# Durations that a hand-written planner uses for matmuls, ScalarE squares and GpSimd operations, and a scratch tile taken out of its ordering

## Chip, core and metric

The kernel runs on one NeuronCore of a Trainium2 chip. The metric is device time in microseconds (us) of that core, from the launch to the end of the program. The profile's own span, from the first to the last instruction of the program, is a little shorter.

## The reference, cut to what matters

Two layers work on a sequence of 256 tokens of width 1024, all in float32. Each layer has three parts, and each part normalises its input, normalises its result and adds it to the residual x:

```
for l in range(2):
    h = rms_norm(x, ln_mix_pre[l]); z = h @ w_in[l]             # 1024 x 7436
    branches = nsa(z), retention(z), rwkv7(z), short_conv(z)    # four token mixers
    merged = sum over m of sigmoid(z_gate[m]) * (branches[m] @ w_branch[l, m])
    x = x + rms_norm(merged @ w_mix_out[l], ln_mix_post[l])
    x = x + rms_norm(cross_attention(rms_norm(x, ...), rms_norm(mem, ...)), ln_xa_post[l])
    h = rms_norm(x, ln_mlp_pre[l])
    x = x + rms_norm(square(relu(h @ mlp_w1[l])) @ mlp_w2[l], ln_mlp_post[l])
```

`rms_norm` needs the mean square of each row, then its power of -1/2. These few numbers stand between the last matmul of one part and the first matmul of the next.

## The kernel before, in words

**Tiling.** Tokens are two tiles of 128 (t = 0 and 1). Weights stream in as units of 128 x 1024 numbers. Each is split by ScalarE (`hi`, rounded to float32r) and VectorE (`lo`, the rest), and each product is three float32r matmuls (`mm3`: hi hi, hi lo, lo hi), of 256 or 512 columns. The second matmul of the MLP uses a seven-product scheme in place of eight; its weights need sums too, one of them made by a DMA that adds (`accumulate`, line 738, issued from GpSimd's queue). The small matmuls of the mixers stay in plain float32, many of them on 64-row tiles, issued in groups (`together`, line 700).

**The planner.** The kernel's program is not issued in the order in which it is written. Each operation is recorded by `Sched.add` with an engine, a duration in us, and dependencies with latencies (`LAT`, `OWN`). `Sched.run` then plays a list schedule: at each step it takes the operation that can start first, by its own clock for PE, ACT, DVE, POOL and DMA; of those that start together, the one of lowest rank. Rank 9 is the stream of large matmuls, rank 0 the chain between two parts, ranks 1 to 5 the mixers and the preparation of memory, "split" a rank that depends on how many units are split ahead of use. The order in which it takes them is the order of the instructions on each engine and on each DMA queue. On the chip every engine works its list in that order and waits at its head. The planned durations are used for nothing else: they leave no trace in the program but the order.

**Durations.** They stand in the helpers: `act` (line 628), `ts` (line 649; on GpSimd where `pool=True`), `rpow` (line 672, a power on GpSimd), `mm` (line 679) and `together`, which adds up its members. In the profile all squares, copies and splits of ScalarE carry line 631, VectorE's tensor_tensor line 642, its scalar_tensor_tensor line 648, tensor_scalar of either engine line 654, GpSimd's power line 676, matmuls line 685 and transposes line 690.

**Scratch tiles.** Tiles of a tag share a number of buffers (`NB`). `Sched.fits` lets an operation start a tile only if all tiles of that tag that stand earlier in the program can still be placed. The tag `junk` has one buffer. It takes the squares themselves, which nobody reads: the sum of squares leaves through the accumulator of the same instruction. With one buffer the rule makes the squares run in the order of the program text, one after another with 0.1 us between them. The squares are in `sumsq` (line 920), `pre_first` and `post_bank` (line 1005).

**A boundary between two parts.** `wide` (the end of a mixer or of cross-attention) and the end of `mlp` finish token tile 0, then token tile 1. For each, `post_bank` squares the result's two banks of 512 columns and multiplies by the gain; `post` forms the power of -1/2 on GpSimd (two operations) and updates x on VectorE (two operations); `pre` multiplies x by the next gain, squares x, and transposes on PE for the next part. In program order tile 0's whole `boundary` stands ahead of tile 1's `post_bank`. While a boundary runs, PE has other matmuls in hand where there are any: in layer 0 the keys of the memory for both layers (`kpairs`; `ftile_whole` in plain float32 at the end of layer 0).

## Time and profile before

| what | value |
|---|---|
| median of 3 runs | 1088.1 us (1085.91 to 1088.32) |
| the profiled execution's own time | 1090.18 us |
| its span, first to last instruction | 1088.1 us |
| PE busy | 98% of the span |
| VectorE, ScalarE, GpSimd busy | 79%, 60%, 9% |
| mean granted TensorE clock | 0.998 |

PE's busy time is made of records that overlap: a matmul's record lasts longer than the distance to the next one's start. So work on PE is read below from starts, and idle PE time in a row is shorter than the stall by what the last record overhangs. Rows of the other engines say when a result was there; a number in square brackets in a row is the idle time of that engine just before it, with what ended it.

### The profile page before, as it was taken

The page shows a single profiled execution, that of the slowest core. Times are in us where ns is not written, and L with a number is a line of the kernel's source. Part 1 is how long each engine was busy: PE and PEld are TensorE (multiplying, and loading weights), DVE is VectorE, ACT ScalarE, POOL GpSimd, SP SyncE. Part 2 cuts the span into 40 slices and gives each one's busy share as a digit, 9 for nine tenths or more (in the row PEclk, how much of TensorE's full clock was granted, in tenths as well). Part 3 has the DMA queues.
Part 4 walks back from the last instruction along what each step waited for, and adds up shares of the span by engine and source line. Part 5 has one row for each costly group of instructions (what it writes and reads, how often), then busy time and mean ns, then how long its engine had stood idle before and what let it go on. Part 6 is the DMA issues. An engine that isn't in the chain of part 4 may idle for free.

```text
span 1088.1 us, 20208 instructions
## 1 busy us (share of the span) xinstructions
PE 1069.9 (98%) x7848; PEld 936.1 (86%) x7848; DVE 856.8 (79%) x1347; ACT 657.5 (60%) x1069; POOL 96.1 (9%) x154
## 2 busy tenths in 40 slices
PE   8999999999999999999999999999999999999997
PEld 7989877888998899999889998778888987999996
DVE  6867887866767689888796767977867667999997
ACT  7574655645555667776665664644546455776673
POOL 2000011001100110000020000100002002000000
PEclk9999999999999999999999999999999999999999
DMA  8546555755546699998945257356645467889981
GB/s 328 164 128 183 210 174 165 266 186 169 170 157 218 212 273 288 267 279 254 298 165 172 79 160 254 126 174 201 237 164 173 149 224 210 255 267 293 270 265 51
DMA packets 75970, 225.18 MB, mean 207 GB/s; under 512 B 12223, under 2 KB 14015, under 8 KB 75748
## 3 DMA queue, kind: packets, MB, share of 16 engines
q1 hardware_dynamic: 71268, 207.65, 55.7%
q0 software_dynamic: 4320, 15.73, 8.8%
q8 instruction: 61, 1.00, 0.4%
q10 hardware_dynamic: 288, 0.52, 0.2%
q14 instruction: 33, 0.27, 0.1%
HBM read 221.77 MB, written 3.15 MB: 207 GB/s over the span
## 4 chain that ended last, share of the span: by engine, by line
PE 88%; DMA 3%; DVE 3%; issue 2%; ACT 2%; POOL 2%; SPq 0%; POOLq 0%; DVEq 0%; ACTq 0%
PE A L685 47%; PE C L685 18%; PE S L685 12%; PE B L685 8%; DMA g<-wts 2%; PE C L690 2%; DVE g L642 1%; POOL s L654 1%; DMA raw<-wts 1%; ACT junk L631 1%; DVE lo L642 1%; DVE x L648 1%; ACT g L631 1%; PE B L690 0%; POOL s L676 0%
## 5 line engine op out<-in xcount | busy, mean ns | idle before, releaser
L642 DVE TENSOR_TENSOR lo<-raw,hi 128x1024 fp32r<-128x1024 f32 (+1 forms) x308 | 368.4, 1213 | 70.2 <-ACT hi L631 41.8
L631 ACT ACTIVATE hi<-raw 128x1024 fp32r<-128x1024 f32 (+1 forms) x308 | 316.2, 1049 | 136.7 <-PE A L685 67.1
L685 PE MATMUL A<-hi,g 128*128 128x512 f32 (+2 forms) x1152 | 370.3, 389 | 0.9 <-ACT g L631 0.5
L685 PEld LDWEIGHTS A<-hi,g 128*128 128x128 f32 x1152 | 214.5, 188 | 48.1 <-issue 4.3
L685 PE MATMUL A<-lo,g 128*128 128x512 f32 (+2 forms) x576 | 220.2, 382 | 0.0
L642 DVE TENSOR_TENSOR g<-g,g 128x512 f32<-128x512 f32 (+3 forms) x218 | 187.9, 886 | 9.8 <-ACT g L631 8.5
L631 ACT ACTIVATE g<-g 128x512 fp32r<-128x512 f32 (+7 forms) x228 | 149.0, 693 | 43.3 <-DVE g L642 19.6
L685 PE MATMUL A<-g,hi 128*128 128x256 f32 x928 | 169.2, 285 | 0.0
L685 PE MATMUL C<-g,hi 128*128 128x256 f32 x960 | 167.7, 278 | 1.1 <-ACT g L631 1.1
L685 PEld LDWEIGHTS C<-g,hi 128*128 128x128 f32 x960 | 147.4, 188 | 3.7 <-ACT g L631 1.5
L685 PEld LDWEIGHTS A<-g,hi 128*128 128x128 f32 x928 | 141.2, 188 | 5.2 <-issue 3.4
L685 PE MATMUL C<-g,lo 128*128 128x256 f32 x480 | 133.5, 278 | 0.0
L685 PE MATMUL A<-g,lo 128*128 128x256 f32 x464 | 129.1, 278 | 0.0
L631 ACT ACTIVATE g<-C 128x512 fp32r<-128x512 f32 (+5 forms) x119 | 59.4, 513 | 110.8 <-PE C L685 84.6
L685 PEld LDWEIGHTS A<-lo,g 128*128 128x128 f32 x576 | 108.4, 188 | 17.5
L685 PE MATMUL S<-g,g 128*128 128x512 f32 x450 | 108.3, 391 | 0.3 <-DVE g L642 0.3
L685 PEld LDWEIGHTS S<-g,g 128*128 128x128 f32 x450 | 84.3, 188 | 19.0 <-DVE g L642 0.8
L685 PEld LDWEIGHTS C<-g,lo 128*128 128x128 f32 x480 | 91.0, 190 | 0.0
L685 PEld LDWEIGHTS A<-g,lo 128*128 128x128 f32 x464 | 87.3, 188 | 0.2 <-DVE lo L642 0.2
L631 ACT ACTIVATE g<-A 128x512 f32<-128x512 f32 (+3 forms) x70 | 39.5, 567 | 54.4 <-PE A L685 42.3
L654 POOL TENSOR_SCALAR s<-s 128x1 f32<-128x1 f32 (+1 forms) x38 | 27.3, 719 | 349.8 <-ACT junk L631 297.1
L642 DVE TENSOR_TENSOR g<-C,g 128x512 fp32r<-128x512 f32 (+3 forms) x66 | 37.0, 587 | 23.7 <-ACT g L631 17.3
(144 smaller groups left out, 1079.0 us busy)
## 6 DMA issues: line engine op xcount, KB each, us to landing
raw<-wts SPq DMA_DIRECT2D x300, 512.0 KB, 4.7
g<-wts SPq DMA_DIRECT2D x90, 256.0 KB, 5.3
g<-wts POOLq DMA_DIRECT2D x30, 512.0 KB, 5.7
g<-rows SPq DMA_DIRECT2D x11, 512.0 KB, 4.7
g<-memT SPq DMA_DIRECT2D x12, 256.0 KB, 6.9
g<-cmpw SPq DMA_DIRECT2D x4, 512.0 KB, 4.5
raw<-wts SPq DMA_DIRECT2D x4, 498.0 KB, 6.2
raw<-wts SPq DMA_DIRECT2D x4, 480.0 KB, 6.2
```

What stands on the lines that cost most here:

```text
L631: e = lambda: self.nc.scalar.activation(real(out), real(in_), func, bias=real(bias), scale=real(scale), accum_out=real(accum))
L642: f = lambda: e.tensor_tensor(real(out), real(a), real(b), op)
L648: f = lambda: self.nc.vector.scalar_tensor_tensor(real(out), real(a), real(s), real(b), op0=op0, op1=op1)
L654: f = lambda: e.tensor_scalar(real(out), real(a), real(s1), real(s2), op0=op0, **kw)
L685: e = lambda: self.nc.tensor.matmul(real(out), real(lhsT), real(rhs), start=start, stop=stop, skip_group_check=True)
L690: self.pe(0.109, out, [in_, self.ident], lambda: self.nc.tensor.transpose(real(out), real(in_), real(self.ident)), 128)
```

## The change

Four kinds of edits. (1) The planned durations: a float32r matmul takes n/2240 in place of n/2400 + 0.002 us; a group with 64-row operands takes 0.25 us more; a tensor_scalar on GpSimd 0.7 in place of 0.15; a power on GpSimd 0.1 more. (2) An ACT operation takes 0.01 more, 0.19 more where it accumulates (0.064 before), and nothing more for a scale or bias from a tile (0.064 and 0.096 before, and 0.042 more when the input is in SBUF). (3) The scratch tile of the squares becomes one fixed tile with its own place. (4) Writes into it make no dependency (`sink`). No operation is added or removed, and none works on other data.

```diff
-NB = {..., "g1": 5, "junk": 1, "s": 14, "x8": 6,
+NB = {..., "g1": 5, "s": 14, "x8": 6,
@@ class VT
+        self.sink = False
@@ Sched.add
         for v in op.outs:
             t = v.t
+            if t.sink:
+                continue
@@ act
-        cost = 0.08 + self.free(out) / 1200 + 0.064 * n + (0.042 if n and not in_.t.psum else 0.0)
+        cost = 0.09 + self.free(out) / 1200 + 0.19 * (accum is not None)
@@ ts, on GpSimd
-            return self.s.add("POOL", 0.15 + self.free(out) / 800, [out], [a, s1, s2], f)
+            return self.s.add("POOL", 0.7 + self.free(out) / 800, [out], [a, s1, s2], f)
@@ rpow
-        return self.s.add("POOL", 0.25 + 0.2 * n, [out], [a], f)
+        return self.s.add("POOL", 0.35 + 0.2 * n, [out], [a], f)
@@ mm
-            c = max(n, 252) / 2400 + 0.002
+            c = max(n, 252) / 2240
-            c = max(n, 128) * 4 / 2400 + 0.003
+            c = max(n, 128) * 4 / 2400 + 0.004
@@ together
-            cost = i = 0
+            cost, i = 0.25 * (g[0][1].shape[0] == 64 or g[0][2][0].shape[0] == 64), 0
@@ setup
+        self.junk = self.keep([128, 512], "junk", BF16)
+        self.junk.t.sink = True
@@ sumsq, pre_first, post_bank
-            j = self.tile([128, 512], "junk", BF16)
+            j = self.junk
```

## Rows read from the trace of the kernel before

**Rows 1.** The page: busy time, share of the span and instructions of each engine.
```profile
PE 1069.9 (98%) x7848; PEld 936.1 (86%) x7848; DVE 856.8 (79%) x1347; ACT 657.5 (60%) x1069; POOL 96.1 (9%) x154
```

**Rows 2.** Busy time of each engine by stage. Columns: the stretch, its length, PE, PEld, DVE, ACT and POOL busy with their instructions, granted clock, DMA share, GB/s. In order: the mixers of layer 0; its gated sums; the end of layer 0's MLP into layer 1; the mixers of layer 1; the MLP of layer 1; the end.
```profile
9.00:180.00 171.00, 171.00 (x1727) 146.61 (x1727) 136.05 (x275) 105.89 (x204) 13.92 (x29) 1.00 0.57 190
180.00:262.00 82.00, 82.00 (x372) 67.35 (x371) 57.65 (x71) 41.53 (x57) 2.67 (x5) 1.00 0.62 212
...
540.00:580.00 40.00, 38.17 (x221) 33.35 (x220) 35.05 (x45) 26.58 (x47) 8.08 (x9) 1.00 0.62 214
580.00:740.00 160.00, 159.26 (x1628) 135.73 (x1629) 121.45 (x255) 90.62 (x176) 10.80 (x19) 1.00 0.48 154
...
922.00:1078.00 156.00, 156.00 (x1019) 142.25 (x1018) 142.90 (x198) 109.86 (x151) 11.21 (x13) 1.00 0.82 242
1078.00:1089.00 11.00, 2.05 (x15) 1.76 (x13) 6.08 (x11) 2.47 (x8) 2.71 (x5) 0.71 0.25 95
```

**Rows 3.** The chain that ended last, in the MLP of layer 0. Columns: start, length, engine, tile and line, number of pieces.
```profile
417.41 5.45 PE C L685 x48
422.87 4.78 PE S L685 x21
...
438.13 5.45 PE C L685 x48
```

**Rows 4.** Timeline of PE where the MLP of layer 0 ends and layer 1 begins. Columns: start, length, engine, line, operation, out<-in, form, count, idle time before and who ended it. B<-g,raw are the keys of layer 1 in plain float32; C<-g,g are the transposes of token tile 0, then of tile 1.
```profile
552.44 5.34 PE L685 MATMUL B<-g,raw 128*128 128x256 f32 x24
557.62 2.03 PE L685 MATMUL C<-g,g 128*128 128x128 f32 x16
559.48 5.34 PE L685 MATMUL B<-g,raw 128*128 128x256 f32 x24
566.17 2.05 PE L685 MATMUL C<-g,g 128*128 128x128 f32 x16 [1.34 <-DVE g L654]
568.06 3.62 PE L685 MATMUL B<-g,raw 128*128 128x256 f32 x16
```

**Rows 5.** Timeline of POOL in the same stretch, token tile 1.
```profile
558.02 1.42 POOL L654 TENSOR_SCALAR s<-s,s 128x1 f32<-128x1 f32 x1 [0.80 <-ACT junk L631]
559.52 0.56 POOL L676 TENSOR_TENSOR s<-s,mhalf 128x1 f32<-128x1 f32 x1
563.34 1.81 POOL L654 TENSOR_SCALAR s<-s 128x1 f32<-128x1 f32 x1 [3.26 <-ACT junk L631]
565.23 0.56 POOL L676 TENSOR_TENSOR s<-s,mhalf 128x1 f32<-128x1 f32 x1
```

**Rows 6.** Timeline of DVE in the same stretch: the two operations beside GpSimd's first and fourth row of the group above, and what PE waited for.
```profile
558.06 1.22 DVE L642 TENSOR_TENSOR lo<-raw,hi 128x1024 fp32r<-128x1024 f32 x1
...
563.85 1.22 DVE L642 TENSOR_TENSOR lo<-raw,hi 128x1024 fp32r<-128x1024 f32 x1
565.83 0.29 DVE L654 TENSOR_SCALAR g<-ident,s 128x128 f32<-128x128 f32 x1 [0.77 <-POOL s L676]
```

**Rows 7.** All tensor_scalar operations of POOL on one small tile (line 654): shortest, median and longest in ns, first and last start, forms.
```profile
L654 POOL TENSOR_SCALAR s<-s x38: 196/440/1807, 7.0 to 918.5; 128x1 f32<-128x1 f32 x34, 128x8 f32<-128x8 f32 x4
```

**Rows 8.** Timeline of PE at the transposes of token tile 1, from the mixer of layer 0 into its cross-attention, and from that into its MLP. B<-g,hi are keys of the memory.
```profile
274.88 0.28 PE L685 MATMUL B<-g,lo 128*128 128x256 f32 x1
275.38 0.66 PE L690 MATMUL C<-ident,g 128*128 128x128 f32 x4 [0.22 <-DVE g L642]
...
379.40 0.66 PE L690 MATMUL C<-ident,g 128*128 128x128 f32 x4 [0.21 <-DVE g L642]
```

**Rows 9.** Timeline of PE from the cross-attention of layer 1 into its MLP, where no keys are left.
```profile
907.37 1.26 PE L690 MATMUL C<-ident,g 128*128 128x128 f32 x8 [0.47 <-DVE g L642]
...
909.78 0.51 PE L685 MATMUL A<-hi,g 128*128 128x512 f32 x1 [0.47 <-ACT g L631]
...
910.91 0.74 PE L685 MATMUL A<-hi,g 128*128 128x512 f32 x2 [0.40 <-DVE g L642]
...
917.24 1.60 PE L690 MATMUL C<-ident,g 128*128 128x128 f32 x12 [1.01 <-DVE g L642]
```

**Rows 10.** Timeline of ACT in the same stretch. junk<-x squares token tile 0's x, junk<-A the two banks of token tile 1.
```profile
906.02 0.63 ACT L631 ACTIVATE junk<-x 128x512 bf16<-128x512 f32 x1 [3.10 <-DVE x L648]
...
909.16 1.06 ACT L631 ACTIVATE g<-C 128x512 fp32r<-128x512 f32 x2
910.11 0.59 ACT L631 ACTIVATE junk<-A 128x512 bf16<-128x512 f32 x1
...
911.63 0.59 ACT L631 ACTIVATE junk<-A 128x512 bf16<-128x512 f32 x1
```

**Rows 11.** Timeline of PE at the end of the rwkv mixer of layer 1, and at the first products of the MLP of layer 0.
```profile
676.38 0.63 PE L690 MATMUL B<-ident,g 128*128 128x128 f32 x4 [0.60 <-DVE g L642]
...
406.84 0.50 PE L685 MATMUL C<-g,hi 128*128 128x256 f32 x2 [1.11 <-ACT g L631]
```

**Rows 12.** Groups of ACT by form: two of 128 x 256 with the scale from a tile, and without. Columns: busy us, mean ns of one, idle time before.
```profile
L631 ACT ACTIVATE g<-g 128x256 f32<-128x256 f32 x62 | 23.1, 408 | 0.6
...
L631 ACT ACTIVATE g<-g,pct 128x256 f32<-128x256 f32 x12 | 5.5, 499 | 0.9 <-DVE g L648 0.8
```

**Rows 13.** The chain that ended last, in its last 6 us.
```profile
1081.84 1.04 POOL s L654
```

More of the change, by code (lines that the diff above doesn't have):

```diff
@@ L225, in body @@
         Prog(nc, tc, sb, ps, dr, wts, x, mem, memT, pc, rows, r256, cmpw, cmpe, relb, lora, cst, out, dbg).run()
-NB = {"raw": 5, "hi": 8, "lo": 8, "g8": 7, "g4": 12, "g2": 13, "g1": 5, "junk": 1, "s": 14, "x8": 6,
+NB = {"raw": 5, "hi": 8, "lo": 8, "g8": 7, "g4": 12, "g2": 13, "g1": 5, "s": 14, "x8": 6,
       "p1": 1, "tok1": 1, "tok2": 1, "lk": 1, "ng": 1}
@@ L991, in pre_first @@
                 self.red(acc[:, 0:1], sq, OP.add)
-                j = self.tile([128, 512], "junk", BF16)
+                j = self.junk
                 self.act(j, x[:, 512:], AF.Square, scale=D ** -0.5, accum=acc[:, 1:2])
@@ L1010, in post_bank @@
         cs = cs or slice(512 * i, 512 * i + 512)
-        j = self.tile([128, 512], "junk", BF16)[:, :cs.stop - cs.start]
+        j = self.junk[:, :cs.stop - cs.start]
         self.act(j, bank, AF.Square, accum=acc[:, i:i + 1])
```

## The prediction

> **What bounds the kernel now.** I read the page's busy times first: PE 98%, the next engine 79% [rows 1]. A busy PE is not proof of a full one, so I then read the stages [rows 2]: through the mixers of layer 0 (171 us) and the gated sums (82 us) PE has no idle time at all, in the mixers of layer 1 0.74 of 160 us, in the second MLP none of 156 us. Third, the chain of waits in the MLP, to see the pace of that full PE [rows 3]: from 417.41 to 438.13 are two rounds of 48 matmuls of 256 columns and 21 of 512, so 10.36 us a round. The reader is to see two things there. PE's work is fixed, and the order cannot shorten it. And the planner's old prices, 256/2400 + 0.002 = 0.1087 us and 512/2400 + 0.002 = 0.2153 us, make 48 x 0.1087 + 21 x 0.2153 = 9.74 us of that round, 6% too little; the new ones, 0.1143 and 0.2286, make 10.29 us. The price is now right to 1%.
>
> So what the change can win is idle PE: 1088.1 - 1069.9 = 18.2 us [rows 1], of which 8.1 are the tail (10.1 from 1078 us to the end of the span, less 2.05 of work [rows 2]) and 5.8 the nine waits in [rows 4, 8, 9, 11]. Fourth, therefore, the timelines around these stalls. A stall is read from start to start: a record of 256 columns overhangs the next start by 0.17 us (0.28 long, next start 0.11 later), so a stall is its idle time plus about 0.17.
>
> **The change part by part.** No instruction is added or taken away, no DMA either; everything acts through order. Each term is a stall that the order makes.
>
> *GpSimd prices.* The mean power chain at a boundary is a tensor_scalar and a power. The planner gave 0.15 and 0.45 us; it now gives 0.70 and 0.55. Into layer 1 PE ran 24 records of keys, tile 0's transposes, 24 more keys, stood for 1.34 us (stall 1.51), ran tile 1's transposes, and only then the last 16 records of keys, 3.62 us [rows 4]. The filler was there, but queued behind the transposes, because the planner thought that tile 1's x would be ready sooner. Its two GpSimd pairs took 1.42 + 0.56 and 1.81 + 0.56 us [rows 5], 4.35 in all, against 1.20 planned: 3.15 short. The new prices plan 2.50 and are 1.85 short. The plan's chain grows by 1.30, and by 0.09 for each of two squares, and a group of keys is 4 records, 0.9 us of the 3.62; so one or two groups move ahead of the transposes. I take 1.3 us of the 1.51; bounds 0 and 1.5.
>
> The same at the transposes of tile 1 into the first cross-attention and the first MLP: idle 0.22 and 0.21 us, stalls 0.39 each with the overhang, and keys follow at both [rows 8]. One GpSimd pair stands in each chain, so the plan grows by 0.65, more than the stall. I take both, 0.8 us; bounds 0 and 0.8. At the end of layer 1's rwkv mixer a pair stands in the chain too, PE waits 0.60 idle [rows 11], and the gated sums' matmuls are there as filler: 0.5 us; bounds 0 and 0.8.
>
> Here row and rule differ about the price itself. The tensor_scalar took 196 to 1807 ns, median 440 [rows 7], and the long ones end just behind a VectorE subtraction of 1.22 us: the 1.42 us one at 559.44, the `lo` beside it at 559.28; the 1.81 us one at 565.15, its `lo` at 565.07 [rows 5, 6]. No single number fits that; at a boundary 1.4 to 1.8 is near, off it 0.2 to 0.4.
> The Trainium skill (SBUF — State Buffer, Who interferes with whom) says that a VectorE instruction with two inputs in SBUF keeps out a GpSimd instruction that reads SBUF, and that whichever is issued first keeps the port to its end. The trace agrees that GpSimd waits the subtraction out, though its row starts 0.04 us ahead of it at 558.02; by that rule the price would hang on the neighbour, one group of keys (0.9 us) would move in place of 1.3 us, and the sum below would be 3.4.
>
> *The squares set free.* Into the last MLP there are no keys left, and PE waits four times: 0.47, 0.47, 0.40 and 1.01 us idle [rows 9]. The last is tile 1's transposes. Tile 1's first bank was squared at 910.11 and its second at 911.63, though ACT had stood idle 3.10 us until 906.02, when the squares of tile 0's x could begin [rows 10]. The order of the text put those ahead. Set free, the first bank's square goes into that idle time, and 0.59 us leave ACT's queue ahead of the second; the chain of tile 1 (two GpSimd operations, two on VectorE, the gain) starts that much earlier. I take 0.6 us of a stall of 1.18; bounds 0 and 1.2. The first three waits are tile 0's chain, which no square precedes that could move: nothing. Next late there is that chain. At the other boundaries the same gain is covered by the keys, and counts within the terms above.
>
> *Matmul prices.* With matmuls 5 to 6% dearer the plan hides DMA, splits and chains behind fewer of them; loads and splits keep their pace, which follows units used. Where PE waits for the MLP's first factors, 1.11 us idle [rows 11], the plan sees PE later by 6% and may take the splits in a better order, or not: bounds 0 and 1.3, half of it, 0.6 us. In the mixers it costs a reserve: until now PE in truth came 5% later to each small group than planned, so the group's inputs were nearly always there; now it comes as planned. The 0.25 us for 64-row groups acts in the same way. I cost this at nothing, since the planner's latency of 0.2 us between engines is still in every step; its bounds come under the rivals.
>
> *ACT prices.* A plain operation of 128 x 256 took 408 ns and one with its scale from a tile 499 [rows 12]; the old price had 0.106 for that difference of 0.09, the new one nothing. The new square is 0.09 dearer. The 12 in that group are spread over mixers where PE never waits: nothing, with bounds of -0.5 and +1 us (12 x 0.09).
>
> *The end.* The last GpSimd sum takes 1.04 us [rows 13] where 0.2 to 0.4 is the lower half of [rows 7]; what VectorE runs beside it depends on the order of tile 0's updates. Nothing, bounds -0.7 and +0.7.
>
> **Sum.** 1.3 + 0.8 + 0.5 + 0.6 + 0.6 = 3.8 us less. The profiled execution took 1090.18 us, with a span of 1088.1; it gives 1086.4. It lies 2.1 above the median of the runs, 1088.1, and taken from that the forecast is **1084.3 us**, 0.35% less. A measurement of this kernel can tell some 0.3%, 3.3 us, from no change.
>
> **The rivals.**
>
> *The stalls move and don't go* (within 3.3 us). Filler put ahead of one stall is missing behind it, where ACT still has to split the transposed x; and where GpSimd's operation is held up by VectorE, 0.70 is still short by 0.7 to 1.1 us each. For it: the stall into layer 1 is one of two chains whose plan stays 1.85 us short. Against it: 3.62 us of keys were left there. With half of the terms, 1.9 us, it gives 1086.2; nothing at all gives 1088.1. The variant that the change does not do what it says, since the order comes out nearly the same, ends here too: most of the time is MLP and gated sums with no idle PE [rows 2].
>
> *PE arrives too early in the mixers* (slower). The place is the rwkv chains between 20 and 135 us and between 580 and 690 us, some 225 us in the mixer stages of [rows 2], in which small groups alternate with large matmuls on PE. The price: the planner used to fill a chain's waiting time with 5.2% more matmul time than it knew (0.1143 against 0.1087). If chains run longer on the chip than planned, PE now stands at their groups: at most 5.2% of 225 = 11.7 us, half of it, 5.8, where every other step is late. It decides once a chain step is planned shorter than it runs: GpSimd beside VectorE is (up to 1.8 for 0.70), ACT with a scale is by 0.09 [rows 5, 12]. Against it: PE has no idle time there now, with a reserve of which only half is given up. It gives 1088.1 + 5.8 = 1093.9 us.
>
> **How the numbers follow.** Forecast, faster by more than 3.3 us: 0.43, since four of its five terms are stalls with filler in hand or a named delay, but it clears the bound by 0.5 us only. Moved stalls: 0.35. Early PE: 0.22. The lower end takes all named stalls, 1.5 + 0.8 + 0.8 + 1.2 + 1.3 = 5.6, the end's 0.7, ACT's 0.5 and the three waits of tile 0 with two more of their size elsewhere, 3.8: 1088.1 - 10.6 = 1077.5. The upper end is the slower rival's 1093.9, of whose case the worse half stays out. The likeliest case alone runs from 1077.5 to 1084.8.
>
> **What would show it.** After the change: 1 or 2 more groups of B<-g,raw ahead of tile 1's transposes into layer 1, and less than 0.4 us idle before them in place of 1.34; the square of tile 1's first bank ahead of the squares of tile 0's x, ACT idle under 2.5 us there in place of 3.10, and 0.4 us idle before the last transposes in place of 1.01; the MLP's round unchanged at 10.36 us; PE busy in the mixers without idle time. The forecast is wrong if PE's idle time ahead of the tail stays near 10.1 us (18.2 less 8.1), or if the mixers or their matmuls' starts spread by more than 3 us: then the planner's old error was a reserve. It is wrong in its reason if the time falls but PE idles as before and the end is shorter.

## The result, and the profile after

| | before | after |
|---|---|---|
| median of the runs shown beside each other | 1088.21 us (1085.91 to 1089.23, 4 runs) | 1101.42 us (1096.89 to 1104.61, 4 runs) |
| profiled execution, its span | 1090.18, 1088.1 us | 1102.74, 1100.9 us |

The ratio is 1.0118 with a 95% interval of 1.0096 to 1.014: the change makes the kernel 13 us slower, where 4 us less were forecast and 1093.9 us was the upper end. The runs also spread wider, over 7.7 us.

Busy time by stage of the changed kernel, with the columns of [rows 2], in four of its stretches, the last one longer: the mixers of layer 0; the end of layer 0's MLP into layer 1; the MLP of layer 1; the end.

```profile
9.00:180.00 171.00, 169.31 (x1717) 145.30 (x1718) 138.86 (x281) 105.44 (x204) 14.24 (x28) 1.00 0.54 185
...
540.00:580.00 40.00, 37.59 (x192) 32.91 (x191) 29.50 (x39) 21.88 (x38) 7.55 (x8) 0.96 0.57 196
...
922.00:1078.00 156.00, 151.73 (x992) 137.65 (x991) 140.86 (x195) 108.75 (x153) 15.49 (x16) 0.99 0.87 248
1078.00:1101.00 23.00, 14.90 (x71) 12.27 (x70) 14.63 (x23) 6.16 (x16) 2.71 (x5) 0.88 0.12 46
```

The reader is to see the third row. The last MLP had no idle PE before, 156.00 of 156.00; now 4.3 us of it are idle, and in two stretches (540 to 580, 922 to 1078) the mean granted clock is under 1. To place the loss, I compare the start of the n-th matmul record in both traces; each has 7848. Behind record 120 the changed kernel is late by 1.8 us, behind 1950 (layer 0's mixers done) by 3.5, at 3000 by 2.8, at 3750 (layer 0's MLP near its end) by 5.3, at 4200 (layer 1 begun) by 7.4, at 6900 (last MLP begun) by 7.0, at 7800 by 12.8. So the start costs 1.8 us, layer 0's mixers 1.7, the rounds of the first MLP 2.4, its end with the boundary 2.1, **the last MLP 5.8**, and the rest gives back 1.1.

That last figure is the kernel before's own execution: the profiled one lies 2.1 us above the median of its runs. In experiment 12 below PE, ScalarE, VectorE and GpSimd work in the same order as in the kernel before everywhere outside the two MLPs, and its trace is 0.2 us ahead of the kernel before's at record 1950 and 3.9 us at 6900. Against it the changed kernel gives nothing back: the start costs 2.0 us, layer 0's mixers 1.7, its sums and cross-attention 0.3, its MLP 1.9, the boundary 3.3, layer 1's mixers 1.7, the last MLP 5.3 (16.2 in all, as that execution is a short one of 1086.48 us).

What happens in an MLP round shows in three timelines of the changed kernel: ScalarE, then PE, then the DMA issues of POOL and SP. Columns: start, length, engine, line, operation, tiles, form, count, idle time before and who ended it. `g<-g` of 128x1024 are the splits of U and W (U is what the accumulating DMA writes, W is summed from it by VectorE), `g<-C` is the relu that empties the bank for the next `up`.

```profile
991.32 1.06 ACT L634 ACTIVATE g<-g 128x1024 fp32r<-128x1024 f32 x1 [3.17 <-DMA g<-wts]
993.72 1.06 ACT L634 ACTIVATE g<-g 128x1024 fp32r<-128x1024 f32 x1 [1.34 <-DVE g L645]
994.68 1.04 ACT L634 ACTIVATE hi<-raw 128x1024 fp32r<-128x1024 f32 x1
995.63 0.58 ACT L634 ACTIVATE g<-C 128x512 f32<-128x512 f32 x1
```

```profile
992.68 1.10 PE L688 MATMUL S<-g,g 128*128 128x512 f32 x4
996.26 0.50 PE L688 MATMUL C<-g,hi 128*128 128x256 f32 x2 [2.49 <-ACT g L634]
```

```profile
982.63 0.85 POOL L741 DMA_DIRECT2D g<-wts  x1 [9.54 <-DMA g<-wts]
```

```profile
982.85 0.33 SPq L731 DMA_DIRECT2D raw<-wts  x1
983.23 1.72 SPq L731 DMA_DIRECT2D g<-wts  x3
```

PE's last matmul into C started at 988.65, so the relu could have run at about 989. It stood fourth in ScalarE's queue: behind U's split, which stood 3.17 us at the head for the accumulating DMA (issued at 982.63), behind W's, which waited 1.34 us for VectorE, and behind a `hi`. PE ran out of other products and stood for 2.49 us. In the kernel before the relu of the same round comes first, as soon as PE has finished, and the splits of U (982.77) and W (984.03) follow, before PE needs the bank at 986.88:

```profile
982.28 0.60 ACT L631 ACTIVATE g<-C 128x512 f32<-128x512 f32 x1 [2.69 <-PE C L685]
982.77 2.31 ACT L631 ACTIVATE g<-g 128x1024 fp32r<-128x1024 f32 x3
```

The accumulating DMA is also later than before: in the last MLP the median from issue to landing is 7.8 us where it was 5.5 (rows of the DMA issues of 925 to 1085 us, the kernel before first, then the changed one):

```profile
g<-wts POOLq DMA_DIRECT2D x13, 512.0 KB, 5.5
...
g<-wts POOLq DMA_DIRECT2D x14, 512.0 KB, 7.8
```

The long stall has a tail. Three windows of the changed kernel, before, in and behind a stretch of half clock:

```profile
990.00:996.50 6.50, 4.01 (x19) 2.98 (x18) 5.12 (x6) 3.84 (x5) 0.86 (x1) 1.00 0.84 260
996.68:1000.09 3.41, 3.41 (x18) 3.41 (x17) 3.39 (x7) 2.55 (x5) 0.00 (x0) 0.50 1.00 262
1000.20:1003.60 3.40, 3.40 (x31) 3.40 (x31) 3.40 (x6) 2.30 (x3) 0.00 (x0) 1.00 0.94 331
```

PE was idle for 2.49 of the 6.5 us ahead; then the granted clock was 0.50 (1.2 GHz) for 3.41 us, with 18 matmuls, nearly all of them of 256 columns as in the next stretch, which has 31. So 13 of 31 are missing, some 1.4 us of work. The second such stretch lies behind the other long stall, at the boundary into layer 1 (566.60 to 570.01 us).

There PE, answering to [rows 4], and POOL, answering to [rows 5]:

```profile
557.04 7.07 PE L688 MATMUL B<-g,raw 128*128 128x256 f32 x32
566.51 3.68 PE L688 MATMUL C<-g,g 128*128 128x128 f32 x16 [2.41 <-DVE g L657]
```

```profile
561.65 1.69 POOL L657 TENSOR_SCALAR s<-s,s 128x1 f32<-128x1 f32 x1 [1.97 <-ACT junk L634]
563.42 0.85 POOL L679 TENSOR_TENSOR s<-s,mhalf 128x1 f32<-128x1 f32 x1
564.37 0.85 POOL L657 TENSOR_SCALAR s<-s 128x1 f32<-128x1 f32 x1
565.30 0.84 POOL L679 TENSOR_TENSOR s<-s,mhalf 128x1 f32<-128x1 f32 x1
```

It is now tile 0's transposes that wait, behind 32 records of keys, 2.41 us idle where tile 1's waited 1.34 us. POOL takes tile 1's first pair (561.65) ahead of tile 0's second (564.37). And the whole chain began late, in the same way as in the MLP: the first operation of the end, the copy `g<-S`, is behind two `hi` splits that waited 3.76 us for their DMAs (before, it ran at 544.01). How much of the 2.41 us is this and how much the order on POOL, no run separates.

```profile
547.94 1.06 ACT L634 ACTIVATE hi<-raw 128x1024 fp32r<-128x1024 f32 x1 [3.55 <-DMA raw<-wts]
549.22 1.06 ACT L634 ACTIVATE hi<-raw 128x1024 fp32r<-128x1024 f32 x1 [0.21 <-DMA raw<-wts]
550.18 0.58 ACT L634 ACTIVATE g<-S 128x512 f32<-128x512 f32 x1
```

**Why the plan does this.** The code's own prices say it. Per MLP round the plan charges the DMAs 3 x 1.54 us for units, 0.77 for half a unit, 2 x 0.77 for the halves of U and 3.08 for the accumulating one: 10.02 us. The round's matmuls were 9.74 us at the old price and are 10.29 at the new. So the plan's round was bound by its DMAs and is now bound by PE. While DMAs bound it, a split was planned for when its data came, and the relu was ready by then. With PE the bound, the planned DMAs run ahead, and so do the planned splits, by 4 us and more ahead of the relu. On the chip they do not run ahead: U's split above waited 3.17 us for its data. The plan also gives out the buffers, by the time at which it has one free, so a moved price moves tiles to other buffers as well as other places in the queues (the planned durations do not act through the order alone); no run separates the two. The account so far, a relu held in ScalarE's queue, is theory 1; theory 2 is the recorded rival (PE too early in the mixers); theory 3 puts the loss at the boundary, on the squares or the POOL prices.

### The profile page after: what moved, and what is told of

It reads as the page before. It is cut to its first block, busy times and chain, and to the rows that moved or that the text cites. A ratio compares the mean times of both kernels' runs of the same rounds, so it can differ in the third digit from the quotient of the medians.

```text
span 1100.9 us, 20238 instructions
## 1 busy us (share of the span) xinstructions
PE 1077.6 (98%) x7848; PEld 942.1 (86%) x7848; DVE 859.3 (78%) x1347; ACT 656.9 (60%) x1069; POOL 94.5 (9%) x154
## 4 chain that ended last, share of the span: by engine, by line
PE 77%; DVE 9%; DMA 6%; issue 4%; ACT 2%; POOL 1%; SPq 0%; DVEq 0%; POOLq 0%; ACTq 0%
PE A L688 46%; PE C L688 13%; PE B L688 9%; PE S L688 7%; DVE g L645 6%; DMA g<-wts 4%; DVE lo L645 2%; PE C L693 2%; ACT g L634 2%; DVE g L651 1%; DMA raw<-wts 1%; DMA g<-cmpw 1%; ACT hi L634 1%; PE B L693 0%; DMA x<-x 0%
## 5 line engine op out<-in xcount | busy, mean ns | idle before, releaser
L634 ACT ACTIVATE g<-g 128x1024 fp32r<-128x1024 f32 (+7 forms) x228 | 152.2, 694 | 103.1 <-DVE g L645 59.5
L688 PE MATMUL A<-g,hi 128*128 128x256 f32 x928 | 171.5, 286 | 0.6 <-DVE g L651 0.5
L688 PEld LDWEIGHTS C<-g,hi 128*128 128x128 f32 x960 | 148.3, 190 | 10.1 <-ACT g L634 8.3
L741 POOL DMA_DIRECT2D g<-wts x30 | 26.4, 879 | 319.7 <-DMA g<-wts 147.1
```

What stands on the lines that cost most here:

```text
L634: e = lambda: self.nc.scalar.activation(real(out), real(in_), func, bias=real(bias), scale=real(scale), accum_out=real(accum))
L688: e = lambda: self.nc.tensor.matmul(real(out), real(lhsT), real(rhs), start=start, stop=stop, skip_group_check=True)
L741: f = lambda: self.nc.gpsimd.dma_start(real(out), in_, accum_op=OP.add)
```

## The experiments

"Round" counts MLP rounds from 0. A stall of PE "by starts" is its idle time plus the 0.16 to 0.17 us that the last record overhangs; where a text says idle, it is the idle time alone. Stalls come from one profiled execution each. Stalls "ahead of C" are those of the kind above, released by ScalarE's relu, and are given by starts.

**1. The changed kernel, relu first from round 6 on.** Only the plan's order is tied; no wait of the chip is added.

```diff
 def up(j)
-            self.act(r, p, AF.Relu)
+            self.relus.append(self.act(r, p, AF.Relu))
 def wpair(l, j)
+        if j > 5:
+            as_[2].deps.setdefault(self.relus[-2 + j // 14], -9.0)   # U's split
```

> The changed kernel with one order put back: in MLP rounds 6 to 14 the split of U on ScalarE may not go ahead of the relu of the next `up`. Theory 1 (a split that waits for the accumulating DMA blocks the relu, and PE waits for the relu's bank): the stalls of the MLPs, 1.1 + 1.3 us in layer 0 and 0.3 + 2.7 + 0.4 + 0.9 us in layer 1, go, with the half-clock window of 3.4 us behind the longest (1.7 us): 1093 to 1095 us, and no stall of PE over 0.5 us inside the rounds. Theory 2 (PE arrives too early in the mixers): the loss lies there, 1100 to 1102 us. Theory 3 (the end of layer 0's MLP and the boundary hold the loss): also over 1099 us.

1093.59 us, ratio to before 1.0061 (1.004 to 1.0082). By the medians 8 of the 13 us are back, by the ratios 6. In the last MLP the relu runs at once and no stall ahead of C is left; ScalarE, then PE, one round further on:

```profile
995.23 0.60 ACT L634 ACTIVATE g<-C 128x512 f32<-128x512 f32 x1 [2.19 <-PE C L688]
995.72 2.00 ACT L634 ACTIVATE g<-g 128x1024 fp32r<-128x1024 f32 x2
```

```profile
996.40 3.56 PE L688 MATMUL S<-g,g 128*128 128x512 f32 x15
999.80 0.40 PE L688 MATMUL C<-g,hi 128*128 128x256 f32 x2
```

The accumulating DMA still took 7.9 us there (median); with the relu ahead that cost nothing. The stalls left are in rounds of layer 0 that were not tied (1.44 us at 429, 1.79 at 451); none over 0.5 us was expected.

**2. The kernel before, relu behind U's split.** The same tie, the other way round (`self.relus[-2 + j // 14].deps.setdefault(as_[2], -9.0)`).

> The kernel before with all its old prices, and one order reversed: in MLP rounds 6 to 14 the relu of the next `up` goes behind the split of U. Theory 1: it loses in the MLPs what the change loses there, 5 to 9 us: 1093 to 1097 us, with stalls of PE ahead of the matmuls into C, released by ScalarE. Theories 2 and 3: within 1 us of before, 1087 to 1089 us; no price moved.

1087.21 us, ratio 0.9995 (0.9982 to 1.0009). Theory 1 as put failed here: this order alone costs nothing that can be told.

**3. The matmul price alone** (the two lines of `mm`).

> Of the change only the price of matmuls. Theory 1: the relu goes behind the split in rounds 6 to 14 of both layers as in the whole change, so the MLPs lose 5 to 9 us; with the mixers' small stalls (some 3 us in layer 0) 1094 to 1099 us. Theory 2: the mixers' 3 us and nothing in the MLPs, 1090 to 1092 us. Theory 3 (squares or POOL prices at the boundary): 1088 us, no loss at the boundary into layer 1.

1106.54 us (1101.12 to 1112.84), ratio 1.0175 (1.0126 to 1.0223). The price alone loses 18.7 us, more than the whole change. Waits for the relu in the last MLP, in us, times and longest:

```profile
PE C L685 <- ACT g L631: 7.7, 5, 2.4
```

By starts they are 8.5 us, with half clock behind two of them. The boundary loss is there too, though squares and POOL prices are the old ones: ahead of tile 0's transposes PE was idle for 2.69 us. So theory 3 falls. Another 4.3 us of its trace go between records 6000 and 6900, where PE was idle for 1.86 us ahead of the transposes of layer 1's cross-attention, with half clock behind it; the whole change loses nothing there, and why the price alone does is open.

**4. All but the matmul price.**

> The change without the price of matmuls. Its planned order has the relu first in rounds 6 to 13 of layer 0 and behind the split in layer 1. Theory 1: no stalls in the rounds of layer 0, those of layer 1 of 3 to 6 us: 1091 to 1094 us, plus what the boundary takes. Theory 2: mixers as before, 1086 to 1088 us. Theory 3: the boundary into layer 1 still costs its 2 to 3 us, 1090 to 1091 us.

1087.86 us, ratio 0.9997 (0.9984 to 1.001). No stall ahead of C in either MLP, also not in layer 1, where the relu was planned behind U's split and 3 to 6 us were expected. Layer 0 up to record 1950 is 4.3 us late; from there to record 7800 its trace gains 5.0 us on the kernel before's, of which some 2 are that execution's own.

**5. The whole change with a dearer accumulating DMA** (`n / 130e3` in `accumulate`).

> The whole change, and the accumulating DMA priced 4.0 us in place of 3.1 (n / 130e3 for n / 170e3), so that in the plan the DMAs and not PE bound an MLP round again (10.97 against 10.78 us in layer 0). In the planned order the relu of the next `up` then goes ahead of U's split in all rounds. Theory 1 (the dearer matmul let splits of late DMAs go ahead of the relu): no stall over 0.5 us in the rounds of either MLP, 1089 to 1093 us. Theory 2 (PE arrives too early in the mixers) and any theory in which the matmul price itself costs: as the change, 1099 to 1103 us.

1094.22 us, ratio 1.006 (1.0039 to 1.008), 1.2 us over the range expected and 7.2 under the changed kernel. The last MLP is full again:

```profile
922.00:1078.00 156.00, 156.00 (x1018) 142.35 (x1018) 141.67 (x196) 110.87 (x153) 12.35 (x15) 1.00 0.83 245
```

With DMA over PE in the plan, the matmul price does no harm in the MLP. What is left lies in the start and the mixers of layer 0 (3.7 us late at record 1950).

**6. Half of the matmul price** (`max(n, 252) / 2330`).

> The kernel before with the matmul price raised by half of the way and nothing else (n / 2330, 0.110 and 0.220 us). The plan is still bound by the DMAs in an MLP round (10.02 against 9.98 us), and U's split leads the relu by 0.9 us in the plan, where it leads by 4.2 to 6.7 with the full price. Theory 1: no loss in the MLPs, 1087 to 1090 us. A loss in proportion to the price, as theory 2 has it: half of the 18.7 us of the price alone, 1096 to 1098 us.

1090.2 us, ratio 1.0022 (1.0009 to 1.0036): no stall ahead of C, and 3.2 us late at record 1950. Not in proportion: half of the price, under the 10.02 us of the DMAs, takes 2.4 of 18.7 us.

**7. POOL prices and squares alone.**

> Of the change only the POOL prices and the squares set free. The terms that the prediction gave them were 1.3 us into layer 1, 0.8 us at the cross-attention and the first MLP, 0.5 us at the end of a mixer and 0.6 us into the last MLP: 1084 to 1086 us if they hold and the matmul price alone spoiled them. If stalls only move: 1087 to 1089 us. If the freed squares or the longer planned POOL chains harm the boundaries: over 1090 us.

1087.63 us, ratio 0.9994 (0.9983 to 1.0005). This lies where "stalls only move" was put. Into layer 1 the trace has what the prediction wanted: under 0.1 us idle ahead of either tile's transposes. It has lost 3.5 us by record 1950 and gains 5.6 from there to 7800, of which some 2 are the kernel before's own execution; experiment 9 tells the two stretches apart.

**8. Relu first from round 2 on** (`j > 1` in experiment 1).

> As the run with the relu put first, but from MLP round 2 on in place of 6. Theory 1: the two stalls that were left in layer 0, 1.44 us at 429 and 1.79 us at 451, go too: 1089.5 to 1091.5 us. If they have another cause: 1093 to 1094 us.

1093.18 us, ratio 1.004 (1.0025 to 1.0056). The two stalls at 429 and 451 are gone, but in the profiled execution the transposes into layer 1 stand longer (1.71 us by starts, 0.56 in experiment 1), and the median moves by 0.4 us alone, where 2 to 4 were expected.

**9 to 11. POOL prices and squares from the end of layer 0's mixers on**, both, the squares alone, POOL alone. A flag is set where `mix` of layer 0 has its merged branches; the plan up to there is that of the kernel before.

```diff
 mix
+        self.late = self.junk.t.sink = True
 ts, on GpSimd (rpow alike)
-        0.15 + self.free(out) / 800
+        (0.7 if self.late else 0.15) + self.free(out) / 800
```

> The POOL prices and the squares set free, but only from the end of layer 0's mixers on; the planned order of everything before that is that of the kernel before. Theory A (both edits give back stalls at the boundaries, 1 us into layer 1, some 0.6 us into the last MLP and some small ones, and with them in force from the start a reordered mixer stage of layer 0 takes 2 to 3 us of it away again): 1083.5 to 1085.5 us, the gated sums of layer 0 reached within 0.5 us of before. Theory B (stalls only move): 1087 to 1089 us.

> The squares alone set free, from the end of layer 0's mixers on. The prediction gave them 0.6 us into the last MLP: 1086.5 to 1087.5 us, nothing at the boundary into layer 1, where the stall of 1.5 us stays. If they harm: over 1089 us.

> The POOL prices alone, from the end of layer 0's mixers on. The prediction gave them 1.3 us into layer 1, 0.8 us at the first cross-attention and the first MLP and 0.5 us at the end of layer 1's rwkv: 1084.5 to 1086 us, the stalls of 1.51 and 0.39 us gone. If the filler moved is missed behind the stall: 1087 to 1088.5 us.

| from layer 0's mixers on | median | ratio to before |
|---|---|---|
| both | 1084.71 us | 0.9974 (0.9963 to 0.9984) |
| squares | 1086.05 us | 0.9986 (0.9973 to 0.9999) |
| POOL prices | 1087.48 us | 0.9998 (0.9989 to 1.0006) |

Both together win 3.3 us by the medians (1.7 to 4.0 by the interval), as expected, and beat both kernels. The squares came out 0.4 us under their range. PE into layer 1, to be read against [rows 4]:

```profile
556.51 1.95 PE L689 MATMUL C<-g,g 128*128 128x128 f32 x16
558.29 5.35 PE L689 MATMUL B<-g,raw 128*128 128x256 f32 x24
563.70 2.05 PE L689 MATMUL C<-g,g 128*128 128x128 f32 x16
565.59 1.89 PE L689 MATMUL B<-g,raw 128*128 128x256 f32 x8
```

No idle time over 0.1 us is left ahead of the transposes. POOL alone cuts that stall from 1.34 to 0.56 us idle but moves the median by 0.5 us only, less than can be told; for POOL the expectation of stalls gone without filler missed elsewhere was a miss. The squares were expected to leave that stall, and did (1.43 us idle).

**12. The kernel before, relu behind the splits of U and W** (`as_[3]` in experiment 2).

> The kernel before with its old prices, and in MLP rounds 6 to 14 the relu of the next `up` behind the split of W too, not of U alone (in the plan 3.4 to 6.6 us behind U's split, as in the change). Theory 1 in its sharper form (the relu must wait behind both splits, since W's waits for VectorE, which waits for the accumulating DMA): stalls of PE at most of the 18 rounds, 0.5 to 2.5 us each, 1096 to 1110 us. Theory 2 or any theory in which a price costs elsewhere: 1087 to 1089 us.

1089.93 us, ratio 1.0017 (1.0005 to 1.0029): the order that the change has, and 1.9 us in place of 8 to 22. Theory 1 in its sharper form falls as well. The profiled execution is one of 1086.48 us; 8 of 10 runs lay at 1089.2 to 1091.0, two at 1086.3 and 1086.5. So its trace can't show where the eight lost their 3 us. It shows ScalarE so:

```profile
986.68 1.06 ACT L631 ACTIVATE g<-g 128x1024 fp32r<-128x1024 f32 x1 [0.70 <-DMA g<-wts]
988.47 1.06 ACT L631 ACTIVATE g<-g 128x1024 fp32r<-128x1024 f32 x1 [0.72 <-DVE g L642]
989.44 1.04 ACT L631 ACTIVATE hi<-raw 128x1024 fp32r<-128x1024 f32 x1
990.39 0.58 ACT L631 ACTIVATE g<-C 128x512 f32<-128x512 f32 x1
```

The splits stand ahead of the relu as in the changed kernel, but U's data were there 1.8 us before PE had finished the `up` (988.47), and the relu comes 1.9 us behind it, in time for PE. The accumulating DMA took 5.8 us (median) here, not 7.8. So, it seems, two things have to meet: the relu behind the splits, and the accumulated data later than PE's `up`. The next four runs were to test that.

**13, 14 and 17, 18. Late data, made on purpose.** In the kernel before, a POOL multiplication of U's sum by 1.0, free in the plan, holds up the accumulating DMA; with the relu first, and with it behind both splits.

```diff
 wpair
+        self.ts(t13, t13, 1.0, pool=True).cost = 0.0     # 17, 18: t13[:, 512:]
         self.accumulate(t13, wa)
```

> The kernel before, in its own planned order (relu first in rounds 6 to 14), with a POOL multiplication of t13 by 1.0, which the plan takes as free, between its DMAs and the accumulating one; an accumulating DMA lands 1 to 3 us later. Two conditions (late data and relu behind): late data alone holds U's split and what follows, but not the relu: PE stalls ahead of C nearly nowhere in rounds 6 to 14, some in the early rounds, where the relu stands behind: 1088 to 1093 us. If late data alone is enough: stalls of 1 to 3 us in most rounds, over 1100 us.

> The same multiplication, and the relu behind both splits, as in the run that cost 1.9 us. Two conditions: now both hold, in 18 rounds; stalls of PE ahead of C, released by ScalarE, of 0.5 to 3 us in most of them, at least 8 us over the run with late data and the relu first: 1098 to 1120 us. If order and late data merely add: the 1.9 us more than that run.

> As the run with late data and the relu first, with the multiplication on 512 of the 1024 columns (at 3.7 to 4.7 us for 1024, an estimate of 1.9 to 2.4 us). Two conditions: with the relu first the delay is mostly hidden: 1088 to 1096 us, stalls ahead of C under 3 us in all. If late data alone is enough: over 1098 us.

> The same half delay with the relu behind both splits. Two conditions: at least 5 us over the run with the same delay and the relu first, in stalls ahead of C that ScalarE ends: 1096 to 1108 us. If order and late data merely add: the 1.9 us of the order alone more than that run. If the other run already loses its time at U and W, as with the full delay, the two come out equal and the question stays open.

| columns multiplied | relu first | relu behind both splits |
|---|---|---|
| 1024 | 1139.44 us (ratio 1.0479) | 1137.88 us (1.0461) |
| 512 | 1131.97 us (1.0397) | 1113.72 us (1.0228) |

Both runs with the relu first lie where "late data alone is enough" was put (over 1100, over 1098); that the relu first would be the slower one, no theory expected. The rule "late data costs only where the relu is behind" is refuted as a rule on the time. The place of the stalls does follow the order: by starts, those ahead of C add up to 6.2 and 1.5 us with the relu first (1024 and 512 columns) and to 20.8 and 12.9 with it behind (both MLPs, behind the first round). Waits of PE from 925 to 1085 us, 512 columns, relu first:

```profile
PEld S L685 <- ACT g L631: 4.7, 2, 3.3
...
PEld S L685 <- DVE g L642: 3.3, 2, 2.0
...
PEld C L685 <- ACT g L631: 2.4, 3, 1.4
```

and relu behind:

```profile
PEld C L685 <- ACT g L631: 11.0, 5, 5.3
...
PEld S L685 <- DVE g L642: 2.0, 3, 1.2
```

With the relu first PE waits mostly for U and W themselves (S), with the relu behind for C. But the delay was not the same in the two: the POOL row of 128x512 took 3.1 us on average in the one and 2.1 in the other, where 1.9 to 2.4 were estimated. The medians are alike, 1.8 and 1.9; five of 30 took 8.0 to 10.3 us in the first, one 7.2 in the second (last section). So the pair does not measure what a common delay costs in either order.

**15. The matmul price in the two MLPs alone.**

> The matmul price raised in the two MLPs alone; U's split leads the relu by 4 to 5 us in the plan there. If the MLPs lose by themselves: 6 to 12 us, 1094 to 1100 us, and nothing in mixers, sums and cross-attention. If the loss needs the price elsewhere (another phase of buffers at the start of the MLP): within 2 us of before.

1092.87 us, ratio 1.005 (1.0033 to 1.0067): 5.5 us, a little under the 6 to 12 expected, and up to record 3000 its trace loses nothing. Stalls ahead of C behind the first round add to 3.5 us in its trace, and PE is idle for 2.66 us ahead of tile 0's transposes into layer 1. The MLP's price needs nothing outside to lose; of the rest of the price alone's 18.7 us it says nothing.

**16. All but the matmul price, from layer 0's mixers on.**

> All edits but the matmul price, from the end of layer 0's mixers on. With POOL prices and squares alone in that place 1084.7 us were measured. If the ACT price and the surcharge on 64-row groups add nothing: 1084 to 1085.5 us. If the surcharge sets layer 1's groups better: 1082.5 to 1084 us. If they cost: over 1086 us.

1084.46 us, ratio 0.9969 (0.9959 to 0.998): the same as experiment 9. The ACT price and the surcharge on 64-row groups add nothing that can be told.

**Taken together.** Prices of a round's matmuls against 10.02 us of DMAs, the order, and the stalls ahead of C that begin behind the first round, summed over both MLPs of one trace:

| kernel | matmuls / DMAs in the plan, us | relu ahead of U's split, rounds 6 to 14 | stalls ahead of C, us |
|---|---|---|---|
| before | 9.74 / 10.02 | yes | 0 |
| changed | 10.29 / 10.02 | no | 6.7 |
| price alone (3) | 10.29 / 10.02 | no | 8.5 |
| price in the MLPs (15) | 10.29 / 10.02 | no | 3.5 |
| half price (6) | 9.89 / 10.02 | mostly no | 0 |
| all but the price (4) | 9.74 / 10.02 | layer 0 yes, layer 1 no | 0 |
| relu first from 6 (1), from 2 (8) | 10.29 / 10.02 | yes | 3.2 (before round 6), 0 |
| DMA dearer (5) | 10.29 / 10.97 | yes | 0 |
| relu behind U (2), U and W (12) | 9.74 / 10.02 | no | 0 |
| POOL prices, squares (7, 9 to 11, 16) | 9.74 / 10.02 | yes in one layer, mostly no in the other | 0 |
| delayed data (13, 14, 17, 18) | 9.74 / 10.02 | yes, no, yes, no | 6.2, 20.8, 1.5, 12.9 |

Without an added delay, the stalls come where the planned matmuls outweigh the planned DMAs and the relu is not tied ahead, and nowhere else. With experiments 1, 8 and 12 this is a table of two by two, in the last MLP: relu behind and data late (changed, 3): stalls; relu first and data late (1, 8: 7.9 and 8.4 us): none; relu behind and data in time (12: 5.8 us, in the trace that was kept): none; neither (before): none. Experiment 1 shows the order's part, since it tied the order (and what buffers the plan moved with it) and left every price; that the lateness has its part is read from this table, not shown.

## Why the prediction was wrong, step by step

**The step that failed is "Matmul prices".** It said that loads and splits keep their pace, put 0.6 us of gain on it, and asked for "the MLP's round unchanged at 10.36 us". It read [rows 3] rightly: the new price is right to 1%. It did not set that price beside the planner's other price for the same round. With matmuls 6% too cheap the plan was bound by its DMAs, 9.74 against 10.02 us; mending the price tipped it to 10.29 against 10.02, bound by PE, and the splits went ahead of the relu. The DMA's own price was near in the kernel before: an accumulating one is planned to land 5.6 us after its start, 3.08 + 2.5, and took 5.5; only under the new order it takes 7.8. So loads did not keep their pace, and splits held up the relu. Measured: 18.7 us lost by that edit alone, 13 beside the others, 6 to 8 of them undone by moving one relu per round, where 0.6 us of gain stood.

**The rival that should have had the chance** was in neither list: a full PE was taken as nothing to lose. [rows 2] show no idle PE in the last MLP, and DMA busy for 82% of it and VectorE for 142.90 of 156 us. A stage with no idle time has no gain to offer, but it can lose. PE's idle time ahead of the tail went from 10.1 us to 15.3; that it stays near 10.1 was the prediction's own sign of being wrong.

**"PE arrives too early in the mixers"** named the right sign and a real loss in its two places. Layer 0 from record 120 to 1950 takes 204.9 us before and 206.6 after. Layer 1 from 4200 to 6000 takes 196.0 and 196.1, but the 196.0 is one execution: six other traces with the very same order of these mixers (experiments 10, 12 to 14, 17, 18) take 194.4 to 194.6, and the four of kernels with all edits (changed, 1, 5, 8) 196.1 to 196.7. So both places lose some 1.7 us. The price of the matmul by itself is not the cause: POOL prices and squares alone make the layer 0 stretch 207.7, all but the matmul price 207.8; in layer 1 the price alone makes 194.9 and all but the price 194.7. Every set of edits that was tried from the start reorders layer 0's mixers and loses 1.7 to 3.3 us there. Why is open: the loss is spread over many starts. The start itself, 1.8 us late at record 120, is late by more than 1.4 us only in the kernels that have the ACT price and the surcharge there; which of the two is not separated.

**GpSimd prices, 1.3 us into layer 1.** The mechanism was right and the sign came out wrong: with POOL prices and squares alone 32 + 24 records of keys stand ahead of tile 1's transposes in place of 24 + 24, and under 0.1 us of idle time is left. In the whole change, with the matmul price, the end of the MLP comes late, and the idle time is 2.41 us in place of 1.34. With the page of the Trainium skill that the prediction weighed (SBUF — State Buffer, Who interferes with whom) it had 3.4 us for the sum; neither sum came near.

**GpSimd prices at the other places.** The stalls of 0.39 us at the first cross-attention and the first MLP are gone, and so is the one at the end of layer 1's rwkv. For two of the three that is no merit of the prices. Experiments 12, 14, 17 and 18 have the old prices and the order of the kernel before at these places: the stall at the cross-attention is there in each (0.22 or 0.23 us idle), the one at the first MLP and the 0.60 us at the rwkv in none. These two belonged to one execution, and 0.9 us of the forecast stood on them.

**The squares.** Right in kind and size. Into the last MLP, answering to [rows 10] and the last of [rows 9], ScalarE and PE of the changed kernel:

```profile
912.12 0.60 ACT L634 ACTIVATE junk<-A 128x512 bf16<-128x512 f32 x1 [2.06 <-PE A L688]
...
913.44 0.63 ACT L634 ACTIVATE junk<-x 128x512 bf16<-128x512 f32 x1 [0.63 <-DVE x L651]
```

```profile
924.51 0.66 PE L693 MATMUL C<-ident,g 128*128 128x128 f32 x4 [0.69 <-ACT g L634]
```

A bank of tile 1 is squared ahead of tile 0's x, and the last transposes wait 0.69 us in place of 1.01. The stalls there add to 2.3 us from start to start where they were 3.0: 0.7 us, 0.6 forecast. Alone, from layer 0's mixers on, the squares win 2.0 us by the medians (0.1 to 2.9 by the interval); what they win besides the 0.7 is open.

**First MLP factors.** Here the prediction had the mechanism before its eyes and misread it. The 1.11 us of [rows 11] stand ahead of a matmul into C, not at the factors. What ended them is the relu at 406.21, which stood on ScalarE behind splits that had waited 4.76 us for a DMA; PE's last matmul into C had started at 400.68:

```profile
402.51 2.85 ACT L631 ACTIVATE g<-g 128x1024 fp32r<-128x1024 f32 x3 [4.76 <-DMA g<-wts]
405.26 1.04 ACT L631 ACTIVATE hi<-raw 128x1024 fp32r<-128x1024 f32 x1
406.21 0.57 ACT L631 ACTIVATE g<-C 128x512 f32<-128x512 f32 x1
```

So the first round of the kernel before already had the stall that the change brought to later rounds. In the changed kernel it is gone, and two others of 0.53 and 0.57 us by starts stand there, these for the factors: 1.28 us have become 1.10, a gain of 0.2 where 0.6 was forecast.

**ACT prices and the end.** Costed at nothing. From record 7800 on the two traces take the same time, and experiment 16 beside 9 shows nothing for ACT behind the first mixers.

**The range.** The five waits that the lower end takes at 3.8 us are 3.1 by the prediction's own count (0.62 us each by starts); nothing came near that end.

Experiment 9 has the POOL and squares terms together at 3.3 us (1.7 to 4.0) where the prediction had 1.3 + 0.8 + 0.5 + 0.6 = 3.2. The parts do not bear that out: POOL prices alone win 0.5 us where 2.6 stood, the squares alone 2.0 where 0.6 stood. That the sums agree is in good part luck. In the whole change all of it was outweighed by losses in stages that the sum did not contain.

**What stays open.** How much of the MLP loss is the late data and how much the order: in the changed kernel putting the relu first ends the stalls of the tied rounds though the data stay late (7.9 us), in the kernel before the order alone costs 1.9 us, and the runs with delayed data could not hold the delay equal. Why the accumulating DMAs land later is argued, not shown: over the MLPs of twelve traces (before, after, experiments 1 to 9 and 12), an accumulating DMA beside which SP issued nothing from 1.0 us before to 1.5 us after it landed after 5.7 us (median of 178), one with up to 600 KB issued there after 7.1 (91), one with 600 to 900 KB after 7.7 (77), one with more after 9.1 (14); the issues of 982.63 to 984.2 us above are of the third kind. It is not all: with nothing issued beside them, those of the changed kernel still took 6.6 us (median of 10). Open too is what loses the 1.8 us of the start and the 1.7 of each layer's mixers, some 5 of the 13 us.

## What to carry to other kernels

When a planner's price for one engine is mended, set the whole round's prices of every engine beside each other first: if the engine that binds the plan changes, the order of everything in that round can change, and a price that is right by itself can make the plan worse. Read a stage without idle time as one that can only lose, and look there for in-order queues in which something short that frees a buffer can get behind something that waits for a DMA. Look for a stall in a second execution of the same order before a forecast is built on it: two of the nine here were in one execution only. Put such an edit in force stage by stage: POOL prices and squares, which together changed nothing when in force from the start, won 3.3 us once layer 0's mixers kept their order.

## What the runs showed of the hardware that was not expected

**A GpSimd operation of 1.5 to 1.8 us can take 10 us beside VectorE.** POOL in experiment 17, the multiplications of 128x512 in two neighbouring rounds, and VectorE beside the first:

```profile
1035.35 9.55 POOL L654 TENSOR_SCALAR g<-g 128x512 f32<-128x512 f32 x1 [10.69 <-DMA g<-wts]
...
1045.82 1.82 POOL L654 TENSOR_SCALAR g<-g 128x512 f32<-128x512 f32 x1
```

```profile
1034.98 1.82 DVE L642 TENSOR_TENSOR g<-g,g 128x512 f32<-128x512 f32 x2
...
1038.46 2.35 DVE L642 TENSOR_TENSOR lo<-raw,hi 128x1024 fp32r<-128x1024 f32 x2
...
1042.86 0.69 DVE L642 TENSOR_TENSOR g<-g,g 128x512 fp32r<-128x512 f32 x1
```

Of the 30 such operations of experiment 17, the seven beside which VectorE ran no tensor_tensor took 1.5 to 1.8 us; 18 beside one or a few took 1.5 to 3.5, some of them no longer than the first; five took 8.0 to 10.3, each through a train of ten and more of them, which read two inputs from SBUF. The one shown ends 1.35 us after the train's last, at 1043.55, a little less than such an operation takes alone. That VectorE keeps it out is read from these rows; no run changed VectorE's work to test it. The rule of the Trainium skill named above (SBUF — State Buffer, Who interferes with whom), that such a VectorE instruction keeps out a GpSimd one that reads SBUF, agrees in kind; the row shows more, a wait through many instructions. The changed kernel's price of 0.7 us plus the columns is one number for both cases.

**Half clock behind stalls of about 2 us, but not behind all.** In the changed kernel idle times of 2.41 and 2.49 us of PE were each followed by 3.4 us at a granted clock of 0.50, some 1.4 us of work lost behind the second. In experiment 3 the same followed idle times of 1.86, 1.90 and 2.35 us, but not the longest one, 2.69 us, nor the 2.66 us of experiment 15. In experiment 9 such a stretch follows two shorter ones close together, 0.62 and 1.23 us idle (half clock from 905.94 us). The kernel before, with 1.34 us alone [rows 4], has none between 4.08 and 1082.69 us. So the length of one stall does not tell what its clock will cost.
